# A planner's model: VectorE and GpSimd operations kept apart on a shared path, and time for changes between stream and side products

## The chip, the cores and the metric

The kernel runs on one core of a Trainium2 chip. The metric is the time of one execution on the device, in microseconds (us); less is better.

## The reference

One inference step of a trunk of two layers (DEPTH 2), for a prompt of 256 tokens and one new token of each of 8 running samples, in float32. Cut to what matters here:

```python
def trunk_layer(x, ...):                       # x: (tokens, 2048)
    h = rms_norm(x, norm_w)
    z = h @ w_in                               # columns split among three branches
    y_a, wkv_new = rwkv_time_mix(z_a, ...)     # A: 12 heads of 64, state S (64 x 64) per head
    y_b, kv_new = attention_branch(z_b, ...)   # B: dilated windows, QK norm, rotary, caches
    y_c, pool_new = pool_branch(z_c, ...)      # C: means over 2, 4, 8, 16 rows, small products
    return x + concat(y_a, y_b, y_c) @ w_out, ...

def step(S, inp):                              # inside rwkv_time_mix, one token
    r_t, w_t, k_t, v_t, kk_t, a_t = inp
    sa = einsum('bhvk,bhk->bhv', S, -kk_t)
    S = S * w_t + sa * (kk_t * a_t) + v_t * k_t
    return S, einsum('bhvk,bhk->bhv', S, r_t)
```

For the prompt, `step` is computed in chunks by matrix products; for the samples it is one step on the states that come in as `state_wkv` and leave as `s_wkv`. The outputs are the new rows, the new states and the rows to append to the caches.

## The kernel before

All 264 columns (256 tokens and 8 samples) lie side by side, features on partitions. Layer after layer, `Trunk.stream` brings the weights in tiles `raw` of 512 KB (SyncE's DMA, three buffers). ScalarE rounds each to `hi`, VectorE makes the rest, `lo = raw - hi` (three buffers), and TensorE multiplies: 24 products for each `raw`, `hi` by `xh` and `xl` and then `lo` by `xh`, into two of the three PSUM banks `acc`. After four `raw` a pair of output tiles is complete; VectorE scales the two into `z` (`z<-acc,rstd`), and that frees their banks. These 128x264 products are the *stream*.

All other work of TensorE is called *side* here, and goes through five PSUM banks `a` (line L115 for products, L118 for transposes): the scale of the norm (`row_scale`: the Newton chain `nwt`, `rtok` on VectorE, then `dg` and its products), the chunked recurrence of A (`right`, `iv`, `y`, `uv`, `bt`, `gs`, `st`, `ar`), transposes of `z`, `zv` and `tok`, sums over windows (`kh`), the attention. Side products stand between stream products, so TensorE always has something to do as long as what it needs is there in time.

The samples' step (`a_sample`) cuts the states into 8 pieces `s4` with two buffers. For each piece GpSimd clears it (L789) and starts its loads (L158), does three products (L161) and starts the two stores. VectorE does the multiplications with `arows` (L140), the sum `asa` (L152) and its scale (L144), the rank-one update, and the sum `aos`.

Every engine runs its instructions in a fixed order. That order is set when the kernel is built, by the class `Plan`. It takes the instructions of the program, gives each a duration (`cost`), works out what depends on what, and simulates the five engines with a list of ready instructions for each; the one with the longest chain behind it (`tails`) goes first. Between engines it adds a hand-over time (`HOP`) and, for what does not feed the stream directly, a margin of 350 ns. Then `apply` writes the instructions in the order of the simulated starts. So a number in `Plan` costs nothing by itself and can move instructions on all engines. The two buffers of `s4`, the banks of `acc` and `a` and the other pools are counted in the simulation, and an instruction that lacks one is put aside. Instructions that belong together (`bundle`, a row of small products) are claimed as one.

The plan's durations for GpSimd, the last lines of `cost`, and its use of a DMA started by GpSimd in `run`:

```python
ty = type(i).__name__
return 120 + n * 2.2 if ty == "InstTensorTensor" else 140 + n * 3.2 if ty == "InstTensorCopy" else 50 + n * 0.82
...
free[e] = now + 1050
begin = max(now + 1690, bus_free)
```

Of the kernel before, what the change touches and what calls it, by code (L numbers as in the profile page):

```python
# [103 lines left out]
class Trunk:  # L104
    def __init__(self, ctx, tc, ins, outs, depth=DEPTH):
        self.ctx, self.tc, self.nc, self.ins, self.outs, self.depth = ctx, tc, tc.nc, ins, outs, depth
        self.uid = 0
        self.bundles, self.open = [], None
# [1207 lines left out]
def width(a, first=1):  # L1316
    n = 1
    for _, c in list(a.ap)[first:]:
        n *= c
    return n  # L1320


class Plan:


    def __init__(self, tc, bundles):
        self.tc = tc
        self.tiles = {t.name: t for t in tc.tiles}
        self.block = tc.nc.cur_bb.bb
        self.masks = {}  # L1330
        engine = lambda i: ENGINES.get(str(i.engine).split(".")[-1])
        self.ins = [i for i in self.block.instructions if engine(i) and not type(i).__name__.startswith("BassTilePool")]
        self.eng = [engine(i) for i in self.ins]
        self.n = len(self.ins)
        self.dma = [type(i).__name__ == "InstDMACopy" for i in self.ins]
        self.stream = [type(i).__name__ == "InstMatmult" and self.tiles[list(i.outs)[0].bass_ap.tensor.name].tag.startswith("acc") for i in self.ins]
        self.first = self.stream.index(True)
        self.dur = [self.cost(i, e) for i, e in zip(self.ins, self.eng)]
        self.dependences()
        self.bundle(bundles)  # L1340
        self.rings()
        gone, self.phases = [], []
        for i in self.block.instructions:
            if type(i).__name__.startswith("BassTilePool"):
                op, pool = self.boundary(i)
                if op == "alloc":
                    self.phases += [(pool, g) for g in gone]
                else:
                    gone.append(pool)
# [97 lines left out]
    def cost(self, i, e):  # L1447
        aps = [a for a in list(i.ins) + list(i.outs) if getattr(a, "bass_ap", None) is not None]
        if type(i).__name__ == "InstMatmult":
            n, m = width(aps[0]), width(aps[1])  # L1450
            if "float32r" in str(aps[0].dtype):
                return max(121 * n / 264, 109)
            d = max(n, m) * 0.8333 + 2
            if not getattr(i, "is_transpose", False):
                d = 2 * max(n, m) * 0.8333 + 2
                d *= 0.55 if m <= 32 else 0.72 if m <= 64 else 1
            return d
        if type(i).__name__ == "InstDMACopy":
            return 1050.0
        n = max(width(a) for a in aps)  # L1460
        psum = any(a.bass_ap.tensor.name in self.tiles and self.space(a.bass_ap.tensor.name) == "PSUM" for a in aps)
        wide = [a for a in i.ins if getattr(a, "bass_ap", None) is not None and width(a) > 1]
        thin = sum(1 for a in i.ins if getattr(a, "bass_ap", None) is not None and width(a) == 1)
        if e == "DVE":
            if type(i).__name__ == "InstMemset":
                return 8 + n * 1.04
            fast = type(i).__name__ == "InstTensorScalarPtr" and len(wide) == 1 and not psum
            return 69 + n * (0.52 if fast else 1.042) + (60 if thin else 0)
        if e == "ACT":
            return (51 if psum else 93) + n * 0.834 + (93 * thin if n > 1 else 0)  # L1470
        ty = type(i).__name__
        return 120 + n * 2.2 if ty == "InstTensorTensor" else 140 + n * 3.2 if ty == "InstTensorCopy" else 50 + n * 0.82

    def bus(self, i):
        o = list(i.outs)[0]
        run = min(a.ap[-1][1] * 4 if a.ap[-1][0] == 1 else 4 for a in list(i.ins) + list(i.outs))
        return width(o, 0) * 4 * (1.0 if run >= 512 else 2.0 if run >= 128 else 2.46 if run >= 64 else 8) / 360.0
# [27 lines left out]
    def run(self, factor=1, hop=300, margin=200, batch=0, wait=0, switch=0, quiet=0, lead=1, dyn=()):  # L1505
        n, eng, preds, dma, dur, stream = self.n, self.eng, self.preds, self.dma, self.dur, self.stream
# [37 lines left out]
        free = {e: 0.0 for e in names if e != "SIDE"}  # L1544
        hw = bus_free = now = 0.0
        start, fin, order = [0.0] * n, [0.0] * n, {e: [] for e in free}
        release = []
        last_use = defaultdict(float)
        done, since, side_on, last_stream, forced = 0, None, False, False, None
        claims = {k: [t for t in ts if t in left] for k, ts in self.claim.items()}  # L1550
# [28 lines left out]
        while done < n:  # L1579
            while pending and pending[0][0] <= now + 1e-9:  # L1580
                _, k = heapq.heappop(pending)
# [8 lines left out]
            for e in free:  # L1590
                if free[e] > now + 1e-9 or (e == "SP" and hw > now + 700):
                    continue
                if e == "PE" and forced is not None:
                    k = forced
                elif e == "PE":
# [3 lines left out]
                    k = None  # L1599
                    if h:  # L1600
                        go = side_on or h[0][0] < -2e9 or now - since >= wait or sum(dur[x[1]] for x in h) >= batch
                        if go:
                            k = take(h)
# [3 lines left out]
                    if k is None:  # L1607
                        k = take(ready["PE"])
                        if k is None and h:
                            k = take(h)  # L1610
# [3 lines left out]
                else:  # L1614
                    k = take(ready[e])
# [11 lines left out]
                if dma[k]:  # L1627
                    if e == "SP":
                        hw = max(hw, now) + 470
                        free[e] = now + 60  # L1630
                        begin = max(hw + 650, bus_free)
                    else:
                        free[e] = now + 1050
                        begin = max(now + 1690, bus_free)
                    bus_free = begin + bust[k]
                    fin[k] = bus_free + 908
                else:
                    extra = switch if e == "PE" and stream[k] and not last_stream else 0
                    free[e] = fin[k] = now + dur[k] + extra
                if e == "PE":  # L1640
                    last_stream = stream[k]
                    forced = self.after.get(k)
# [32 lines left out]
            now = min(c)  # L1675
# [68 lines left out]
def build(nc, shapes, depth=DEPTH):  # L1744
    ins = {n: nc.dram_tensor(f"in_{n}", s, F32, kind="ExternalInput").ap() for n, s in shapes.items()}
    outs = {n: nc.dram_tensor(f"out_{n}", s, F32, kind="ExternalOutput").ap() for n, s in _OUTS}
    with tile.TileContext(nc, schedule_with_timeline_sim=True) as tc, ExitStack() as ctx:  # L1747
        trunk = Trunk(ctx, tc, ins, outs, depth)
        trunk.run()
        plan = Plan(tc, trunk.bundles)  # L1750
        plan.run(margin=350, hop=180, factor=0.9, lead=25, quiet=60, dyn=[("a", 2)])
        plan.apply()


# [10 lines left out]
```

## Time and profile before

| what | value |
|---|---|
| median of 3 runs | 1121.6 us (1117.91 to 1131.32) |
| the profiled execution | 1119.54 us |
| its span from the first to the last instruction | 1117.8 us |
| mean granted clock of TensorE | 0.983 |
| TensorE busy | 1052.2 us, 94% |
| VectorE busy | 883.3 us, 79% |
| ScalarE busy | 546.3 us, 49% |
| GpSimd busy | 253.9 us, 23% |

Busy time and waits come from one execution, which lies 2.1 us below the median. Names in a row (`acc<-xh,hi`) are the program's tiles, written one and read ones, without their numbers. In rows of single instructions the time in brackets is idle time of the engine just before, and what ended it. Products of float32 are shown as two records each, so an xcount of 24 in such a row is 12 products. A clock of 1.0 is TensorE's full speed, 0.50 half of it.

### The profile page before, as it was taken

The numbers are of one execution on the slowest core, as the hardware profiler recorded it, in microseconds if no ns is written. First come the engines' busy times: TensorE is split into PE (matmuls) and PEld (weight loads), VectorE is DVE, ScalarE is ACT, GpSimd is POOL, SyncE is SP. The second block draws the span as 40 slices with busy tenths as digits, with TensorE's granted clock in tenths as the row PEclk, the third lists the DMA queues.
The fourth block names the chain that finished last, engine by engine and source line by source line (L and its number), as shares of the span: only waits on it lengthen the run. The fifth ranks groups of instructions, "written<-read, shape, count | busy, mean of one in ns | idle before, by whom it ended". The sixth has DMA issues, their size and how long they took to land. (4 is left out here: it accounts for less than half of the span.)

```text
span 1117.8 us, 24655 instructions
## 1 busy us (share of the span) xinstructions
PE 1052.2 (94%) x9802; PEld 1004.6 (90%) x9802; DVE 883.3 (79%) x1665; ACT 546.3 (49%) x928; POOL 253.9 (23%) x391
## 2 busy tenths in 40 slices
PE   8999999879999999999999999989898899989998
PEld 7899999878899987899999998978888898879998
DVE  7768987698999988865665699668899999787443
ACT  6545533445536545454545464334563474544332
POOL 3202310345532310000121132014453422010000
PEclk9999999889999999999999999998999999999999
DMA  7554478966366894577765545887744578655774
GB/s 253 174 172 150 144 247 235 240 149 199 113 198 192 266 290 136 188 219 224 227 224 170 170 140 177 243 251 189 192 151 133 178 236 286 201 189 181 230 226 143
DMA packets 146652, 221.48 MB, mean 198 GB/s; under 512 B 67441, under 2 KB 100609, under 8 KB 146521
## 3 DMA queue, kind: packets, MB, share of 16 engines
q1 hardware_dynamic: 137272, 193.78, 57.5%
q0 software_dynamic: 9264, 26.13, 7.4%
q8 instruction: 77, 1.26, 0.5%
q14 instruction: 39, 0.31, 0.1%
HBM read 197.47 MB, written 22.95 MB: 197 GB/s over the span
## 5 line engine op out<-in xcount | busy, mean ns | idle before, releaser
L137 ACT ACTIVATE hi<-raw 128x1024 fp32r<-128x1024 f32 (+1 forms) x296 | 310.2, 1048 | 398.1 <-PE acc L321 295.0
L321 PE MATMUL acc<-xh,hi 128*128 128x264 f32 x1824 | 476.4, 292 | 25.0 <-ACT hi L137 10.7
L140 DVE TENSOR_TENSOR lo<-raw,hi 128x1024 fp32r<-128x1024 f32 (+1 forms) x296 | 362.2, 1224 | 153.3 <-ACT hi L137 151.4
L321 PE MATMUL acc<-xl,hi 128*128 128x264 f32 x1824 | 475.3, 292 | 3.8 <-DVE xl L149 3.8
L321 PEld LDWEIGHTS acc<-xh,hi 128*128 128x128 f32 x1824 | 348.9, 191 | 33.7 <-ACT hi L137 11.5
L321 PEld LDWEIGHTS acc<-xl,hi 128*128 128x128 f32 x1824 | 349.8, 192 | 10.3 <-DVE xl L149 4.2
L321 PE MATMUL acc<-xh,lo 128*128 128x264 f32 x1824 | 279.3, 289 | 0.0
L321 PEld LDWEIGHTS acc<-xh,lo 128*128 128x128 f32 x1824 | 243.9, 190 | 3.9 <-issue 1.8
L140 DVE TENSOR_TENSOR z<-acc,rstd 128x264 f32<-128x264 f32 (+1 forms) x112 | 51.3, 463 | 19.3 <-PE acc L321 17.2
L351 POOL COPY zcol<-z 128x9 f32<-128x9 f32 x50 | 23.5, 471 | 146.2 <-DVE z L140 142.0
L321 PE MATMUL acc<-mb,hi 128*128 128x264 f32 x384 | 54.8, 285 | 0.0
L321 PEld LDWEIGHTS acc<-mb,hi 128*128 128x128 f32 x384 | 50.1, 189 | 0.0
L321 PE MATMUL acc<-ml,hi 128*128 128x264 f32 x192 | 48.4, 283 | 0.0
L321 PE MATMUL acc<-mh,hi 128*128 128x264 f32 x192 | 48.2, 283 | 0.0
L321 PEld LDWEIGHTS acc<-mh,hi 128*128 128x128 f32 x192 | 36.1, 188 | 0.0
L321 PEld LDWEIGHTS acc<-ml,hi 128*128 128x128 f32 x192 | 36.0, 188 | 0.0
L321 PE MATMUL acc<-mc,hi 128*128 128x264 f32 x256 | 34.5, 286 | 0.1
L321 PEld LDWEIGHTS acc<-mc,hi 128*128 128x128 f32 x256 | 32.5, 188 | 0.6 <-DVE mc L140 0.5
L158 POOL DMA_DIRECT2D resid<-xs x16 | 8.7, 543 | 102.7 <-DVE xs L140 101.5
L321 PE MATMUL acc<-mh,lo 128*128 128x264 f32 x192 | 31.4, 286 | 0.0
L321 PE MATMUL acc<-mb,lo 128*128 128x264 f32 x192 | 31.1, 284 | 0.0
L158 POOL DMA_DIRECT2D vc<-in_cache_v_w x12 | 9.0, 748 | 96.5 <-PE a L115 61.8
(358 smaller groups left out, 1473.5 us busy)
## 6 DMA issues: line engine op xcount, KB each, us to landing
raw<-in_w_in SPq DMA_DIRECT2D x224, 512.0 KB, 4.4
raw<-in_w_out SPq DMA_DIRECT2D x64, 512.0 KB, 3.5
g_dram<-gs SPq DMA_DIRECT2D x8, 768.0 KB
gs<-g_dram SPq DMA_DIRECT2D x8, 768.0 KB, 6.5
kc<-in_cache_k_w POOLq DMA_DIRECT2D x12, 512.0 KB, 6.8
qb<-q_dram SPq DMA_DIRECT2D x12, 512.0 KB, 3.8
vc<-in_cache_v_w POOLq DMA_DIRECT2D x12, 512.0 KB, 4.7
s<-in_state_wkv POOLq DMA_DIRECT2D x32, 96.0 KB, 3.6
```

The lines of the kernel that those rows point to most:

```text
L137: self.nc.scalar.activation(out, in_, func, **kw)
L140: self.nc.vector.tensor_tensor(out, a, b, op=op)
L158: self.nc.gpsimd.dma_start(out, in_)
L321: self.nc.tensor.matmul(accs[t][:, :T], a[:, k4, cs], b[k], start=first, stop=q == order[3] and k4 == 3 and late)
L351: self.nc.gpsimd.tensor_copy(self.zcol[:, :, a], z[:, NP - 1:T])
```

## The change

Four things in the plan's model are new. `shares` marks the instructions that use a path into SBUF which VectorE and GpSimd have in common: on GpSimd every computing instruction with an operand in SBUF, on VectorE those with two wide operands in SBUF, or a copy or scalar operation from SBUF to SBUF. In the simulation a marked instruction on one of the two engines lasts longer by the time that the other's marked instruction still runs. A stream product behind a side product costs 105 ns more, and a side product behind a stream product 52 ns, unless a bundle begins with it. A DMA that GpSimd starts takes 520 ns of its time instead of 1050. A small GpSimd operation (under 100 elements in a row) costs 120 + 2.2 n ns instead of 140 + 3.2 n or 50 + 0.82 n. The arithmetic and the number of computing instructions are the same; only their order changes.

```diff
         self.dur = [self.cost(i, e) for i, e in zip(self.ins, self.eng)]
+        self.port = [self.shares(i, e) for i, e in zip(self.ins, self.eng)]
         self.dependences()
...
         ty = type(i).__name__
+        if ty == "InstTensorTensor" or n < 100:
+            return 120 + n * 2.2
         return 120 + n * 2.2 if ty == "InstTensorTensor" else 140 + n * 3.2 if ty == "InstTensorCopy" else 50 + n * 0.82
+
+    def shares(self, i, e):
+
+        if e not in ("DVE", "POOL") or type(i).__name__ == "InstDMACopy":
+            return False
+        here = [a for a in i.ins if getattr(a, "bass_ap", None) is not None and a.bass_ap.tensor.name in self.tiles
+                and self.space(a.bass_ap.tensor.name) == "SBUF"]
+        if e == "POOL":
+            return bool(here)
+        wide = [a for a in here if width(a) > 1]
+        to = list(i.outs)[0].bass_ap.tensor.name
+        single = type(i).__name__ in ("InstTensorScalarPtr", "InstTensorCopy") and len(wide) == 1 and self.space(to) == "SBUF"
+        return len(wide) > 1 or single
...
         start, fin, order = [0.0] * n, [0.0] * n, {e: [] for e in free}
+        taken = {"DVE": 0.0, "POOL": 0.0}
...
-                        free[e] = now + 1050
+                        free[e] = now + 520
                         begin = max(now + 1690, bus_free)
...
-                    extra = switch if e == "PE" and stream[k] and not last_stream else 0
+                    extra = 0
+                    if e == "PE" and stream[k] != last_stream:
+                        extra = switch if stream[k] else 0 if k in claims else switch / 2
+                    elif self.port[k]:
+                        extra = max(0.0, taken["POOL" if e == "DVE" else "DVE"] - now)
                     free[e] = fin[k] = now + dur[k] + extra
+                    if self.port[k]:
+                        taken[e] = fin[k]
...
-        plan.run(margin=350, hop=180, factor=0.9, lead=25, quiet=60, dyn=[("a", 2)])
+        plan.run(switch=105, margin=350, hop=180, factor=0.9, lead=25, quiet=60, dyn=[("a", 2)])
```

What that does to the order is shown at three places. The first is VectorE at the start of layer 0, in the Newton chain that leads to `dg` (`lo_105` and `lo_114` are the small parts of two weight tiles, `ss`, `nwt` and `rtok` the chain). Before:

```order
L140 TENSOR_TENSOR lo_105_561<-raw_103_558,hi_104_560 128x1024
L146 TENSOR_SCALAR rtok_60_370<-nwt_61_371 128x3
L140 TENSOR_TENSOR nwt_61_371<-rtok_60_370 128x3
L149 SCALAR_TENSOR_TENSOR nwt_61_371<-nwt_61_371,ss_59_365 128x3
L149 SCALAR_TENSOR_TENSOR rtok_60_370<-nwt_61_371,rtok_60_370 128x3
L140 TENSOR_TENSOR nwt_61_371<-rtok_60_370 128x3
L140 TENSOR_TENSOR lo_114_611<-raw_112_608,hi_113_610 128x1024
L149 SCALAR_TENSOR_TENSOR nwt_61_371<-nwt_61_371,ss_59_365 128x3
L149 SCALAR_TENSOR_TENSOR rtok_60_370<-nwt_61_371,rtok_60_370 128x3
L140 TENSOR_TENSOR nwt_61_371<-rtok_60_370 128x3
```

The same place now:

```order
L146 TENSOR_SCALAR rtok_60_370<-nwt_61_371 128x3
L140 TENSOR_TENSOR nwt_61_371<-rtok_60_370 128x3
L140 TENSOR_TENSOR lo_105_561<-raw_103_558,hi_104_560 128x1024
L149 SCALAR_TENSOR_TENSOR nwt_61_371<-nwt_61_371,ss_59_365 128x3
L149 SCALAR_TENSOR_TENSOR rtok_60_370<-nwt_61_371,rtok_60_370 128x3
L140 TENSOR_TENSOR nwt_61_371<-rtok_60_370 128x3
L149 SCALAR_TENSOR_TENSOR nwt_61_371<-nwt_61_371,ss_59_365 128x3
L149 SCALAR_TENSOR_TENSOR rtok_60_370<-nwt_61_371,rtok_60_370 128x3
L140 TENSOR_TENSOR nwt_61_371<-rtok_60_370 128x3
L140 TENSOR_TENSOR lo_114_611<-raw_112_608,hi_113_610 128x1024
```

Two steps of the chain went ahead of `lo_105` and three ahead of `lo_114`; behind `lo_114` stand two steps instead of five, then `dg`.

The second place is VectorE around the evacuation of the pair of tiles `acc_546`, `acc_547` of layer 0, in the middle of the recurrence and of the samples' pieces. Before:

```order
L152 TENSOR_REDUCE var_463_3282<-gsq_464_3286 128x12
L699 COPY uv_450_3177<-a_468_3320 64x6x64 x2
L140 TENSOR_TENSOR z_560_3993<-acc_546_3871,rstd_66_393 128x264
L140 TENSOR_TENSOR lo_571_4042<-raw_569_4039,hi_570_4041 128x1024
L140 TENSOR_TENSOR z_561_3995<-acc_547_3872,rstd_66_393 128x264
L140 TENSOR_TENSOR s4_336_2206<-s4_336_2206,arows_326_2091 112x512
L140 TENSOR_TENSOR st_470_3348<-a_469_3335,st_454_3221 128x384
L152 TENSOR_REDUCE asa_329_2109<-s4_336_2206 112x8
```

The same place now:

```order
L140 TENSOR_TENSOR s4_336_2206<-asa_329_2109,arows_326_2091 112x512
L146 TENSOR_SCALAR nrs_544_3844<-nwt_545_3848 128x24
L140 TENSOR_TENSOR st_470_3348<-st_470_3348,wc_255_1532 128x384
L140 TENSOR_TENSOR s4_336_2206<-s4_336_2206 112x512
L140 TENSOR_TENSOR nwt_545_3848<-nrs_544_3844 128x24
L146 TENSOR_SCALAR var_463_3282<-var_463_3282 128x12
L140 TENSOR_TENSOR s4_336_2206<-s4_336_2206,arows_326_2091 112x512
L140 TENSOR_TENSOR z_560_3993<-acc_546_3871,rstd_66_393 128x264
L140 TENSOR_TENSOR lo_571_4042<-raw_569_4039,hi_570_4041 128x1024
L140 TENSOR_TENSOR z_561_3995<-acc_547_3872,rstd_66_393 128x264
```

All of `s4_336`'s steps, the update of `st` and steps of a norm (`nss`, `nwt`, `nrs`, `var`) now stand ahead of `z_560`; they stood behind it.

The third place is TensorE at the product of `uv` and `bt` of a chunk, a little later. Before:

```order
L321 MATMUL acc_565_4008<-xh_21_176,lo_574_4072 128x264
L321 MATMUL acc_565_4008<-xh_22_177,lo_574_4072 128x264
L118 MATMUL a_612_4305<-cbase_87,tok_74_409 128x128 x4
L118 MATMUL a_634_4380<-cbase_87,tok_74_409 128x128 x4
L115 MATMUL a_476_3420<-uv_457_3254,bt_456_3253 64x64 x12
L115 MATMUL a_478_3436<-uv_457_3254,gs_466_3303 64x64 x12
L115 MATMUL a_478_3436<-st_470_3348,ar_152_906 64x64 x12
L321 MATMUL acc_565_4008<-xh_23_178,lo_574_4072 128x264
```

The same place now:

```order
L321 MATMUL acc_565_4008<-xh_19_174,lo_571_4042 128x264
L115 MATMUL a_476_3420<-uv_457_3254,bt_456_3253 64x64 x12
L118 MATMUL a_563_4003<-cbase_87,z_561_3995 128x128 x2
L115 MATMUL a_478_3436<-uv_457_3254,gs_466_3303 64x64 x12
L115 MATMUL a_478_3436<-st_470_3348,ar_152_906 64x64 x12
L115 MATMUL a_496_3524<-kh_497_3525,blk_483_3486 128x264
```

The products of this chunk stand one weight tile earlier (by `lo_571` instead of `lo_574`), the sums of `kh` follow at once, and the eight transposes of `tok` are gone from here; they stand later.

## Rows read from the trace of the kernel before

**Rows 1.** The page, part 1: busy us of each engine, share of the span, instructions.

```profile
PE 1052.2 (94%) x9802; PEld 1004.6 (90%) x9802; DVE 883.3 (79%) x1665; ACT 546.3 (49%) x928; POOL 253.9 (23%) x391
```

**Rows 2.** Busy time by stretch: us, PE, PEld, DVE, ACT, POOL busy (instructions), PEclk, DMA share, GB/s.

```profile
216.00:284.80 68.80, 60.02 (x984) 55.88 (x983) 61.56 (x94) 34.51 (x66) 35.40 (x45) 0.95 0.62 178
284.80:461.00 176.20, 166.37 (x1496) 154.22 (x1495) 162.05 (x368) 90.35 (x186) 46.93 (x68) 0.99 0.63 199
...
763.00:830.10 67.10, 60.03 (x987) 55.99 (x986) 61.17 (x94) 34.55 (x67) 35.16 (x45) 0.95 0.67 187
830.10:1010.00 179.90, 167.56 (x1509) 155.54 (x1508) 164.67 (x360) 92.14 (x186) 45.33 (x66) 0.99 0.63 196
```

**Rows 3.** TensorE's waits: its line, what it waited for, us in total, times, longest.

```profile
PE acc L321 <- ACT hi L137: 10.7, 4, 3.8
PE acc L321 <- DVE z L140: 7.1, 8, 2.2
...
PE a L115 <- DVE right L149: 5.2, 2, 2.6
PE a L118 <- DVE zv L140: 4.9, 2, 2.8
PE a L115 <- DVE dg L144: 4.5, 2, 2.5
...
PE a L115 <- DVE zv L140: 3.2, 2, 1.7
```

**Rows 4.** VectorE's timeline at the start: start us, length us, engine, line, operation.

```profile
41.40 1.81 DVE L149 SCALAR_TENSOR_TENSOR nwt<-nwt,ss 128x3 f32<-128x3 f32 x1
```

**Rows 5.** VectorE's timeline around and behind the evacuation of `acc_546`, layer 0.

```profile
284.76 0.43 DVE L140 TENSOR_TENSOR z<-acc,rstd 128x264 f32<-128x264 f32 x1 [0.40 <-PE acc L321]
...
286.84 0.91 DVE L140 TENSOR_TENSOR s<-s,arows 112x512 f32<-112x512 f32 x1
...
290.39 1.17 DVE L144 TENSOR_SCALAR asa<-asa 112x8 f32<-112x8 f32 x1
...
296.61 0.16 DVE L144 TENSOR_SCALAR asa<-asa 112x8 f32<-112x8 f32 x1
...
316.27 0.68 DVE L152 TENSOR_REDUCE aos<-s 112x8 f32<-112x512 f32 x1
```

**Rows 6.** GpSimd's timeline at the same place.

```profile
290.24 1.29 POOL L161 TENSOR_TENSOR s<-s 112x512 f32<-112x512 f32 x1
```

**Rows 7.** TensorE's timeline: stream and side, side products of a chunk, stream alone.

```profile
218.59 0.39 PE L321 MATMUL acc<-xh,hi 128*128 128x264 f32 x1
218.82 0.38 PE L118 MATMUL a<-cbase,z 128*128 128x128 f32 x2
218.96 0.37 PE L321 MATMUL acc<-xl,hi 128*128 128x264 f32 x1
...
285.96 0.92 PE L115 MATMUL a<-uv,bt 128*64 128x64 f32 x24
...
288.35 0.87 PE L118 MATMUL a<-cbase,bk 128*128 128x128 f32 x6
...
325.28 0.28 PE L321 MATMUL acc<-xh,hi 128*128 128x264 f32 x1
325.40 0.29 PE L321 MATMUL acc<-xl,hi 128*128 128x264 f32 x1
```

**Rows 8.** Busy time by stretch where PEclk was 0.50; the sum of five.

```profile
304.36:307.77 3.41, 3.41 (x65) 3.23 (x60) 3.41 (x9) 0.51 (x1) 0.00 (x0) 0.50 0.49 143
...
850.49:853.91 3.42, 3.42 (x64) 3.20 (x59) 3.42 (x9) 0.52 (x1) 0.00 (x0) 0.50 0.37 102
sum 20.49, PE 20.29 PEld 19.28 DVE 19.22 ACT 3.08 POOL 5.24; mean PE 4.06 PEld 3.86 DVE 3.84 ACT 0.62 POOL 1.05
```

**Rows 9.** All instructions of one tile, `out_s_wkv`: ns min/median/max, first and last start.

```profile
L158 POOL DMA_DIRECT2D out_s_wkv<-s x32: 502/512/553, 227.2 to 880.3; - x32
```

## The prediction, made before the changed kernel had run

> **What bounds the kernel now.** I read the page first, then the busy time by stretch, then TensorE's waits, then the timelines at the places that the new order touches. TensorE is busy for 1052.2 of 1117.8 us [rows 1], so 65.6 us of idle time is all that a new order can remove, apart from stretches at half clock and the cost of changing between kinds of product. VectorE looks comfortable at 79% [rows 1], but that is a mean: from 216.0 to 284.8 us it is busy for 61.56 of 68.80 us, and in the same place of layer 1 for 61.17 of 67.10 us, and TensorE is least busy just there (8.8 and 7.1 us idle) [rows 2]. There VectorE, in its fixed order, is what ends the waits: of TensorE's waits for products of VectorE, `z` has 7.1 us, `right` 5.2, the two groups for `zv` 4.9 and 3.2 [rows 3]. The longest single item, 10.7 us for `hi`, is ScalarE behind a weight tile that has just landed; the order of the weight loads on SP is the same in both kernels at those places, so that item stays.
>
> **What the change is worth, part by part.** It removes and adds no instruction. What it does to the time is what another order does, so each term is a place where the order differs. The profiled execution took 1119.54 us (span 1117.8), 2.1 us below the median of 1121.6; I sum against 1119.54 and give the forecast in the same terms.
>
> *Start.* The tile `dg` needs a Newton chain of tiny VectorE operations, and TensorE waited 2.5 us for it in layer 0 (the longest of `dg` in [rows 3]). The last five of the chain ran behind `lo_114` and met two GpSimd products there: the first of them took 1.81 us [rows 4] where its neighbours take 0.16. In the new order three of the five, that one among them, stand ahead of `lo_114`, and two stay behind it. The gain lies between 0 (the last two and `dg` meet the same products instead) and 2.5 us (the whole wait). I take the one blocked operation, 1.81 − 0.16: **−1.7 us**.
>
> *Up to the pinch.* I call pinch the point where VectorE evacuates `acc_546` into `z_560` (284.76 us in the trace, and its like at 830 us in layer 1). 21 VectorE instructions that stood behind it stand ahead of it now, most of them steps of the sample pieces `s4_335` and `s4_336`; none went the other way. The first ran at 286.84 us and the last at 316.27 us [rows 5]; their 21 durations add up to 13.5 us. Rows there overlap the next by 0.08 us each, so they hold the engine for 11.8 us. Of that 2.1 us was contention, half of it in one of them: 1.17 us at 290.39 against 0.16 at 296.61 [rows 5]. It began 0.15 us after GpSimd's product of 290.24 us and ended with it [rows 6]. If the plan does keep such pairs apart, 9.7 us is left; if not, 11.8.
>
> On TensorE 48 products come ahead of the same point. 36 of them are the `uv,bt`, `uv,gs` and `st,ar` of one chunk; the like of these took from 285.96 to 288.35 us [rows 7], 2.4 us for as many. The other 12, transposes and pooled sums, are between 0.07 us (two transposes held TensorE from 218.82 to 218.96 us [rows 7]) and twice that: 0.8 to 1.7 us. So 3.2 to 4.1 us of TensorE's later work is done before the pinch. If VectorE recovers none of its idle time, the pinch comes 9.7 − 4.1 = 5.6 to 11.8 − 3.2 = 8.6 us late for the work then left. If it fills all its idle time (68.80 − 61.56 = 7.2 and 67.10 − 61.17 = 5.9 us [rows 2]), the end is 5.6 − 7.2 = −1.6 to 8.6 − 5.9 = +2.7 us. The idle time there is in short pieces behind `hi` and `acc`, and a sample step that is ready can fill about every second one. I take 5.6 less half of the mean idle of 6.6: **+2.3 us a layer**, between −1.6 and +8.6.
>
> *After the pinch.* VectorE has those 9.7 us less to do. Two waits for `zv` and the longest of `z` lie here: 4.9 + 3.2 + 2.2 = 10.3 us for both layers [rows 3], 5.2 a layer. All could go. But by the later point `acc_869` the new order has 52 VectorE instructions, some 16 us by their rows, and 12.5 us of TensorE's side products ahead that were behind, attention's above all, so the room is partly sold again: between 0 and −5.2, taken at half, **−2.6 us a layer**.
>
> *Clock.* In the four stretches TensorE's granted clock was 0.50, its lower level, for 20.5 us in all, which cost 10.2 [rows 8]. One such window lasts 3.4 us and costs 1.7. Those at 304.36 and 850.49 us begin less than 2 us behind the two waits for `zv` (2.1 and 2.8 us [rows 3]). Where the wait goes, I expect the window to go: 0 to −3.4 us, and half, **−1.7**, in line with half of the waits. Others follow the wait for `right`, which only 19 stream matmuls cover now instead of 23, so I leave them.
>
> *Changes of kind.* A stream matmul that is followed by a side product starts it 0.23 us later (218.59 to 218.82 us) instead of the 0.12 between stream matmuls (325.28 to 325.40); side to stream costs nothing more (218.82 to 218.96 for two) [rows 7]. The plan now charges 52 ns for the first and 105 for the second, so its sign is the wrong way round, but it only has to make runs longer. The order has 433 such changes instead of 453, 10 fewer of the dear kind: 10 × 0.1 = **−1.0 us**.
>
> *DMA issue on GpSimd.* The plan's 1050 ns becomes 520. All 32 stores of `s4` took 502 to 553 ns [rows 9], beside a VectorE that was busy nearly throughout, so the new value is right here and the order built on it is feasible: nothing added.
>
> The Trainium skill has a rule against this part (SBUF — State Buffer, "SBUF: two separate sides"): a DMA issued by GpSimd gets no descriptors while VectorE holds the shared ports in its faster mode, and one of about 620 ns takes about 3100 there. By it an issue would come up to 2.5 us later than the plan believes, an estimate from that page, the sample pieces would not be ready in their turn, and the time would be that of the slower rival below. The trace disagrees so far: the longest of the 32 issues took 553 ns [rows 9].
>
> Sum: −1.7 + 2 × 2.3 − 2 × 2.6 − 1.7 − 1.0 = −5.0, so **1114.5 us**; I write 1114. With every bound on one side it would be −2.5 − 3.2 − 10.3 − 3.4 − 1.0 = −20.4 (1099) or +17.2 (1137). Five terms do not all fall together, so this case's own range is 1102 to 1129.
>
> **Rivals.** *The plan becomes true (faster).* If what made the two stretches of each layer idle is mostly that GpSimd blocked VectorE at moments unknown to the plan, an order that knows it loses most of those waits, not half of a few. TensorE idles 8.8 + 9.8 + 7.1 + 12.3 = 38.0 us in these four stretches [rows 2]. Two thirds is 25 us, and with the waits two thirds of the 10.2 us lost to half clock there go [rows 8], 7 us: 32 us in all, **1088 us**. For it: blocked rows of 1 us and more stand right ahead of TensorE's waits for `zv`. Against it: much of the waiting follows chains with no GpSimd in them (`right`, `hi`), and VectorE is nearly full whatever the order.
>
> *VectorE's line becomes the pinch (slower).* Engines run in order. The sample steps now stand ahead of `z_560` and of the `lo` tiles behind it; when one waits for GpSimd's product or for a landing, the stream stands still, because `acc` has three buffers and the next pair of tiles needs `z_560`. If none of VectorE's idle time is recovered, each layer pays 8.6 us, nothing comes back later, and the two longer waits each bring a half-clock window of 1.7 us: 17.2 + 3.4 = 20.6, **1140 us**. It decides where a sample step ahead of `z_560` is not ready when `acc_546` ends; the plan's margins say it is, and before it was the other way round (VectorE waited 0.40 us for `acc` there [rows 5]).
>
> *Nothing that counts.* The waits move to other operations and add up to the same: **1120 us**, as before.
>
> **How the numbers follow.** The forecast 0.50, faster rival 0.18, slower rival 0.17 (0.02 of it by way of late issues), nothing 0.15. A range of 8 in 10 takes in the forecast and the third whole and about half of either rival: **1091 to 1138 us**. A difference of 2% is about what a measurement of this kernel can tell from no change (runs from 1117.91 to 1131.32); that is below 1099 or above 1144. Below lies the faster rival and a little of the forecast's edge, 0.19; above only the end of the slower rival, 0.09; between them 0.72.
>
> **What would show it.** In the profile of the changed kernel: the wait for `dg` at 46 us under 1 us; `z_560` 0 to 9 us later against the stream matmuls done; fewer VectorE rows of `asa` and `s` above 1 us; the waits for `zv` shorter and the window at about 304 us gone; GpSimd's issues still near 510 ns. The forecast is wrong if sample steps on VectorE show waits for GpSimd or DMA ahead of `z_560` (slower), or if TensorE's idle time in the four stretches falls below 20 us (faster).

## The result, and the profile after

The changed kernel is a little slower: median 1131.5 us (1126.82 to 1135.57) against 1123.02 us for the kernel before on the same chips, ratio 1.0076, 95% interval 1.0053 to 1.0099. One of the 15 runs of the kernel before took 1915.98 us, far from all others, and does not count in the ratio. The profiled execution has a span of 1125.0 us, 7.2 more than that of before. First the page of the changed kernel, part 1 [rows 1]:

```profile
PE 1057.5 (94%) x9802; PEld 1008.1 (90%) x9802; DVE 885.1 (79%) x1665; ACT 544.3 (48%) x928; POOL 263.8 (23%) x391
```

TensorE's idle time is 67.5 us (1125.0 − 1057.5), 1.9 more than the 65.6 of before, and its busy time is 5.3 us more: most of what was lost shows as longer products. To see where, I cut both traces at the same stream products (between the cuts a few stand in another order): from the start of product 1200 to the last of the pair `acc_546`, `acc_547` (the pinch), and from there to product 2700; then the like in layer 1. Busy time by stretch, columns as in [rows 2]; the kernel before:

```profile
192.80:285.10 92.30, 79.71 (x1124) 75.36 (x1123) 73.25 (x109) 45.26 (x78) 40.37 (x52) 0.93 0.74 197
285.10:468.50 183.40, 173.57 (x1555) 161.43 (x1555) 168.49 (x379) 94.57 (x193) 46.93 (x68) 0.99 0.64 199
740.60:829.20 88.60, 77.69 (x1118) 73.43 (x1117) 72.08 (x108) 44.20 (x77) 39.79 (x52) 0.94 0.77 205
829.20:1021.40 192.20, 179.87 (x1610) 167.84 (x1610) 174.10 (x379) 98.90 (x196) 45.33 (x66) 0.99 0.62 194
```

The changed kernel:

```profile
192.20:290.80 98.60, 83.93 (x1206) 78.56 (x1206) 84.95 (x127) 48.94 (x86) 58.25 (x66) 0.93 0.67 181
290.80:472.70 181.90, 172.61 (x1471) 160.64 (x1470) 157.35 (x362) 90.61 (x185) 33.50 (x54) 0.97 0.62 200
745.30:842.50 97.20, 83.24 (x1202) 78.67 (x1200) 85.35 (x123) 48.05 (x85) 56.79 (x64) 0.93 0.69 183
842.50:1028.70 186.20, 177.76 (x1528) 165.08 (x1527) 161.64 (x364) 94.28 (x188) 33.41 (x55) 0.99 0.63 201
```

Up to the pinch the stretches grew by 6.3 and 8.6 us, and VectorE works 11.7 and 13.3 us more in them (73.25 to 84.95, 72.08 to 85.35). TensorE works 4.2 and 5.6 us more there too, so its idle time grew by 2.1 and 3.0 us (12.6 to 14.7, 10.9 to 14.0). Behind the pinch the stretches shrank by 1.5 and 6.0 us. So VectorE did run ahead, TensorE waited longer, and only part of what it had done ahead came back. TensorE's waits in the changed kernel [rows 3]:

```profile
PE acc L321 <- ACT hi L137: 11.4, 7, 2.6
PE acc L321 <- DVE z L140: 10.1, 9, 2.9
PE acc L321 <- DVE compb L140: 9.3, 4, 4.9
PE a L115 <- DVE uv L699: 7.3, 7, 2.5
PE a L115 <- DVE dg L144: 4.9, 2, 2.5
...
PE a L118 <- DVE zv L140: 0.2, 1, 0.2
```

In the kernel before, two of these, which [rows 3] leaves out, were shorter:

```profile
PE acc L321 <- DVE compb L140: 6.9, 3, 2.9
PE a L115 <- DVE uv L699: 1.3, 2, 0.7
```

The waits for `right` and `zv` are gone (13.3 us), and `uv`, `z` and `compb` have taken their place (11.4 us more). The longest, 4.9 us for `compb` (the tail of the same evacuation as `z`), shows how. VectorE's timeline in layer 1 ahead of it, in the changed kernel [rows 5]:

```profile
794.33 2.47 DVE L140 TENSOR_TENSOR s<-s,arows 112x512 f32<-112x512 f32 x1
796.72 2.44 DVE L140 TENSOR_TENSOR s<-asa,arows 112x512 f32<-112x512 f32 x1
799.08 0.67 DVE L152 TENSOR_REDUCE asa<-s 112x8 f32<-112x512 f32 x1
799.68 0.58 DVE L140 TENSOR_TENSOR z<-acc,rstd 128x256 f32<-128x256 f32 x1
800.11 0.17 DVE L140 TENSOR_TENSOR compb<-acc,rstd 128x8 f32<-128x8 f32 x1
```

GpSimd at the same time [rows 6], and the stream product that waited:

```profile
794.98 1.26 POOL L161 TENSOR_TENSOR s<-s 112x512 f32<-112x512 f32 x1
796.21 1.18 POOL L161 TENSOR_TENSOR kh<-k,kh 128x264 fp32r<-128x264 f32 x1
797.36 1.25 POOL L161 TENSOR_TENSOR s<-s,arows 112x512 f32<-112x512 f32 x1
...
800.42 0.56 PE L321 MATMUL acc<-xh,hi 128*128 128x264 f32 x1 [4.87 <-DVE compb L140]
```

Two sample steps, 0.68 us each when undisturbed, take 2.47 and 2.44 us while GpSimd's products run; with the sum behind them they stood behind `z` in the kernel before. Now `z` stands behind them in the fixed order, and the stream behind `z`. The wait costs twice: a half-clock window follows it. Those of the changed kernel in the recurrences, two of them and the sum of all seven [rows 8]:

```profile
302.00:308.80 6.80, 6.44 (x80) 5.64 (x79) 5.73 (x8) 2.93 (x6) 0.60 (x1) 0.50 0.38 117
...
800.40:803.80 3.40, 3.38 (x15) 3.35 (x15) 3.40 (x6) 1.06 (x1) 2.62 (x2) 0.50 0.21 36
...
sum 37.40, PE 34.76 PEld 32.39 DVE 34.65 ACT 13.37 POOL 20.68; mean PE 4.97 PEld 4.63 DVE 4.95 ACT 1.91 POOL 2.95
```

In the same two recurrences the kernel before was at half clock for 30.7 us. Behind layer 0's, the changed kernel has one more such window:

```profile
370.30:373.70 3.40, 3.40 (x18) 3.40 (x17) 2.02 (x4) 1.05 (x2) 1.51 (x3) 0.50 1.01 368
```

The other runs agree: the mean granted clock is 0.976 over the 15 runs of the changed kernel, and 0.981 to 0.982 over each of four sets of runs of the kernel before, taken beside the experiments. By an estimate from these figures the clock cost at most 27 us (0.024 × 1131.5) against 20 to 22, so 5 to 7 of the 8.5 us can be clock.

All operations of `asa`'s scale and of the stores [rows 9] in the changed kernel, ns min/median/max, and `asa`'s scale in the kernel before:

```profile
L144 DVE TENSOR_SCALAR asa<-asa x16: 157/1006/3919, 213.3 to 853.4; 112x8 f32<-112x8 f32 x16
...
L158 POOL DMA_DIRECT2D out_s_wkv<-s x32: 502/516/553, 223.4 to 870.4; - x32
```

```profile
L144 DVE TENSOR_SCALAR asa<-asa x16: 157/312/1169, 217.4 to 866.3; 112x8 f32<-112x8 f32 x16
```

To go by this operation, VectorE is blocked by GpSimd more than before, not less: the median of `asa`'s scale was 0.31 us before and is 1.0 now. The order explains that. With the wait in `run` for marked operations taken out, the plan gives the same order, on TensorE, VectorE and GpSimd alike. `shares` compares the memory space with `"SBUF"`, while the tiles' own name for it is `"SB"`, so it marks no instruction at all. Leaving out the new costs of small GpSimd operations leaves VectorE's order as it is too, and changes 36 of 8638 places in TensorE's order and 8 of 391 in GpSimd's; that was not run alone. So VectorE's new order comes from two parts: the charges between stream and side products, and the 520 ns.

### The profile page after: what moved, and what is told of

It is laid out like the page before. It is cut to its first block, busy times and chain, and to the rows that moved or that the text cites. A ratio compares the mean times of both kernels' runs of the same rounds, so it can differ in the third digit from the quotient of the medians.

```text
span 1125.0 us, 24664 instructions
## 1 busy us (share of the span) xinstructions
PE 1057.5 (94%) x9802; PEld 1008.1 (90%) x9802; DVE 885.1 (79%) x1665; ACT 544.3 (48%) x928; POOL 263.8 (23%) x391
## 5 line engine op out<-in xcount | busy, mean ns | idle before, releaser
L321 PE MATMUL acc<-xh,hi 128*128 128x264 f32 x1824 | 473.9, 291 | 32.0 <-ACT hi L137 11.4
L321 PE MATMUL acc<-xh,lo 128*128 128x264 f32 x1824 | 285.5, 292 | 0.6 <-DVE lo L140 0.6
L321 PEld LDWEIGHTS acc<-xh,lo 128*128 128x128 f32 x1824 | 247.0, 192 | 6.8 <-issue 2.8
L140 DVE TENSOR_TENSOR z<-acc,rstd 128x264 f32<-128x264 f32 (+1 forms) x112 | 51.2, 464 | 16.5 <-PE acc L321 14.2
L351 POOL COPY zcol<-z 128x9 f32<-128x9 f32 x50 | 18.5, 369 | 146.6 <-DVE z L140 144.9
L140 DVE TENSOR_TENSOR s<-s,arows 112x512 f32<-112x512 f32 x32 | 25.4, 796 | 5.6 <-DMA rat<-rat_dram 3.5
```

The lines of the kernel that those rows point to most:

```text
L140: self.nc.vector.tensor_tensor(out, a, b, op=op)
L321: self.nc.tensor.matmul(accs[t][:, :T], a[:, k4, cs], b[k], start=first, stop=q == order[3] and k4 == 3 and late)
L351: self.nc.gpsimd.tensor_copy(self.zcol[:, :, a], z[:, NP - 1:T])
```

## The experiments

Every kernel is the whole computation; only numbers of the plan differ, and so the order. Ratios are to the kernel before on the same chip. I count VectorE instructions that stand ahead of a pair's evacuation and stood behind it in the kernel before, less those that went the other way: at `z_560` (the pinch) and at `z_763`, the first pair behind layer 0's recurrence. "Recurrence" is the time from stream product 1200 to 1820 and its like in layer 1, together, in the profiled execution, against 257.3 us before.

| kernel | at `z_560` | at `z_763` | recurrence, us | ratio (interval) |
|---|---|---|---|---|
| port_marked_alone | −25 | −46 | −19.6 | 1.0192 (1.0161 to 1.0222) |
| port_half_alone | −8 | −31 | −12.2 | 0.9992 (0.9969 to 1.0015) |
| port_quarter_alone | −6 | −23 | −14.4 | 0.9904 (0.9873 to 0.9935) |
| port_marked | −19 | −18 | −0.2 | 1.0020 (0.9993 to 1.0047) |
| port_half | 12 | −2 | −16.8 | 0.9951 (0.9924 to 0.9978) |
| margin355 | 0 | 9 | −0.3 | 0.9995 (0.9970 to 1.0020) |
| port_quarter | 12 | 12 | +2.1 | 1.0026 (1.0001 to 1.0050) |
| dma520_alone | 10 | 13 | −0.3 | 0.9977 (0.9951 to 1.0004) |
| switch_alone | 7 | 22 | −1.1 | 0.9996 (0.9974 to 1.0017) |
| charges_52 | 8 | 24 | +8.9 | 1.0036 (1.0009 to 1.0063) |
| stream128 | 17 | 38 | +7.7 | 1.0144 (1.0109 to 1.0179) |
| charges_dma785 | 9 | 40 | +13.9 | 1.0055 (1.0030 to 1.0080) |
| charges_swapped | 19 | 45 | +11.3 | 1.0095 (1.0063 to 1.0127) |
| the changed kernel | 21 | 47 | +9.5 | 1.0076 (1.0053 to 1.0099) |
| changed_margin355 | 21 | 47 | +4.6 | 1.0116 (1.0088 to 1.0144) |
| changed_hold | 39 | 50 | +9.4 | 1.0110 (1.0074 to 1.0147) |
| stream134 | 44 | 59 | | 1.0284 (1.0245 to 1.0323) |

**The two parts alone, the marking made to work, and a control.** The theory was that what stands ahead of `z_560` costs in proportion; the rival, that any other order scatters by as much.

```diff
# dma520_alone, on the kernel before
-                        free[e] = now + 1050
+                        free[e] = now + 520
# port_marked, on the changed kernel (twice)
-self.space(...) == "SBUF"
+self.space(...) == "SB"
# margin355, on the kernel before
-plan.run(margin=350,
+plan.run(margin=355,
```

> The plan with the GpSimd DMA issue at 520 ns and nothing else of the change. Ledger theory (what stands ahead of z_560 on VectorE sets the loss of the recurrence stretch, 4.7 us a layer for 21 instructions): 10 stand ahead here, so about 2.2 us a layer slower, no gain at the start since that order is the old one: 1.004 of before, some 1127 us. Redraw theory (any changed number of the plan gives another order, and its time scatters by half a per cent whatever the ledger says): anywhere from 0.995 to 1.01, with losses in other places than the recurrence stretch.

> The plan with the charges for changes between stream and side products and nothing else. Ledger theory: 7 instructions ahead of z_560, so 1.6 us a layer, less 1 to 2 us at the start, whose new order comes from this part: about 1.002 of before. Redraw theory: 0.995 to 1.01. If the charges are what costs (they are larger for side to stream, which in the trace of before cost nothing), this kernel alone shows the whole 0.76%.

> The changed kernel with the name of the memory space in shares() corrected, so that operations are marked at all (as it stands the test compares with a name that no tile has, and no instruction is marked). 19 VectorE instructions then stand behind z_560 that stood ahead of it in before. Ledger theory: the recurrence stretch is no slower than before and waits for VectorE fall: 0.99 to 1.0 of before. Rival, VectorE is full in that stretch whatever the order: what is not done ahead is done behind, the chain of the samples ends later, and the time stays between 1.003 and 1.012. Fewer VectorE rows of asa above 1 us in either case.

> The kernel before with one number of the plan moved a little, the margin from 350 to 355 ns: a control for how far any redraw of the order moves the time. Ledger theory: VectorE's order up to z_560 is the old one, so the recurrence stretch stays within 1 us and the whole within 0.3%. Redraw theory: it moves by 0.4% or more, in either direction, as much as the change did.

Neither part alone costs anything that can be measured, and together (with the small costs) they cost 0.8%. The proportional theory falls with the first of them: 10 instructions ahead, and no loss in the recurrence. The charges alone don't even save changes between the two kinds: 457 against 453 before. The control fits the ledger, not the scatter, although the two intervals of dma520_alone and margin355 are too wide to tell 0.3%. port_marked came out between its two theories: its recurrences are as long as before, its time is not clearly longer, and, against what I expected, the median of `asa`'s scale is 1.0 us there too.

**Is the loss one of this order, of the sign of the charges, or of the sample pieces?** The threshold theory: nothing is lost up to VectorE's idle time, everything beyond it.

```diff
# charges_swapped, on the changed kernel
-                        extra = switch if stream[k] else 0 if k in claims else switch / 2
+                        extra = 0 if stream[k] else switch
# changed_hold: VectorE's first step on s4_336 (and s4_1437) not before acc_547 is done
+            held[point].append(first)
+            count[first] += 1
```

> The changed kernel with the charges turned round: 105 ns for a side product behind a stream product, which is the change that cost 0.1 us in the trace of before, and nothing for a stream product behind a side one. 19 VectorE instructions ahead of z_560 instead of 21. Threshold theory (what stands ahead of the stream's steps on VectorE costs nothing up to its idle time of some 6 us a layer, about 10 to 14 instructions, and everything beyond): the loss is nearly the whole one, 1.005 to 1.008 of before. Wrong-charge theory (the loss comes from charging the wrong kind of change): 0.995 to 1.001. Redraw theory: anything from 0.995 to 1.01.

> The changed kernel with the margin at 355 ns instead of 350: a redraw of its own order, that leaves 21 instructions ahead of z_560 and changes the later stretches, of layer 1 above all. Threshold theory: the loss of the recurrence stretches stays, 1.005 to 1.010 of before. Redraw theory: the loss is an accident of one order and goes, at least by half, below 1.004.

> The changed kernel, in which the plan may start VectorE's work on s4_336 (and its like of layer 1) only when the stream has finished acc_547. The planner fills the place with other work: 39 instructions then stand ahead of z_560 instead of 21. Threshold theory: more beyond the idle time, so slower than the changed kernel, 1.010 or more of before. Theory of the sample pieces (it is those steps, with their waits for GpSimd, that hold the line): faster than the changed kernel, under 1.005. Redraw theory: no order between the two.

> The kernel before with nothing but the marking of shared operations, with the name of the memory space corrected: 25 VectorE instructions stand behind z_560 that stood ahead of it, and up to 87 later on. Threshold theory: the stream's steps have VectorE to themselves, so the recurrence stretch gets faster, and what was put off must fit behind: 0.99 to 1.0. Rival, VectorE is full whatever the order: the recurrence's own chain comes later, and the time is 1.003 or more of before.

Three more orders with 19 to 39 instructions ahead lose 1.0 to 1.2%: the loss is no accident of one order, the direction of the charges doesn't matter, and with the steps of `s4_336` behind the pinch the planner fills the place with others and loses as much. Two of the three lost more than I expected, and not all of it in the recurrences: these hold 11.3 of the 14.7 us by which the profiled span of charges_swapped is longer, 9.4 of changed_hold's 18.9, and only 4.6 of changed_margin355's 14.3. The rest is not explained. The fourth missed its expectation in an instructive way. With the full wait charged, VectorE's side work goes behind, and the recurrence gets 19.6 us shorter, but the time is 1.9% longer. Its profile, busy time of the stretch behind layer 0 (272.1 us long before, 305.3 here), and TensorE's longest waits in it:

```profile
449.20:754.50 305.30, 282.30 (x2274) 269.71 (x2273) 214.20 (x395) 136.08 (x210) 44.93 (x84) 0.94 0.59 186
```

```profile
PE a L118 <- DVE os L152: 11.1, 3, 4.4
PE a L115 <- POOL comp L444: 2.9, 1, 2.9
PE acc L321 <- ACT mb L137: 2.2, 2, 1.1
```

What was put off isn't done when the stream has read all of the layer's input weights, and the output projection waits for the attention (`os`, then `mb`). So there are two ways to lose.

**TensorE slower in the model, and half doses.**

```diff
# stream134 (and 128), on the kernel before
-                return max(121 * n / 264, 109)
+                return max(134 * n / 264, 109)
# charges_dma785, on the changed kernel
-                        free[e] = now + 520
+                        free[e] = now + 785
# port_half (0.5) and port_quarter (0.25), on port_marked; "alone": without charges and 520 ns
-                        extra = max(0.0, taken["POOL" if e == "DVE" else "DVE"] - now)
+                        extra = 0.5 * max(0.0, taken["POOL" if e == "DVE" else "DVE"] - now)
# charges_52, on the changed kernel
-plan.run(switch=105,
+plan.run(switch=52,
```

> The kernel before with one duration in the plan changed: a stream product counts 134 ns instead of 121. TensorE is slower in the model, and 44 VectorE instructions stand ahead of z_560 that stood behind it, with no charge for changes and the DMA issue at 1050 ns. Threshold theory (any time added to TensorE in the model lets VectorE's side work run ahead of the stream, and beyond VectorE's idle time the stream pays): the recurrence stretches of the two layers lose 8 us or more together, 1.008 of before or more. Rival, the loss needs the DMA issue at 520 ns or the charges: within 0.3% of before.

> The changed kernel with the GpSimd DMA issue at 785 ns, half way: 9 VectorE instructions ahead of z_560, but 40 and 42 at two points of the later stretch, as many as in the changed kernel. Threshold theory with the place in the recurrence stretch: no loss there, 0.997 to 1.003 of before. Rival, what stands ahead in the later, attention stretch costs the time: 1.006 or more.

> The changed kernel with the marking made to work and half the wait charged: VectorE's order against the stream stays near that of before (12 ahead of z_560, 12 behind at the next pair, mixed later). Threshold theory: neither loss, 0.994 to 1.002 of before, and with the 520 ns the better end if knowing the shared path is worth anything. Rival, charging the shared path hurts at any size: 1.003 or more.

> The kernel before with the marking made to work and half the wait charged, nothing else: 8 VectorE instructions behind z_560 and up to 48 behind later, about half of the full charge. If the cost of the other side is work that spills out of the layer's recurrence and attention (the full charge lost 1.9%, after it had gained 20 us in the recurrence stretches), half the shift should keep part of the gain and little of the spill: 0.99 to 1.005. If every put-off instruction costs: about 1.009.

One number that makes TensorE slower in the model, with nothing of the change, loses 2.8%. That this is the same mechanism at a larger dose is not shown: its one profile, of the slowest of its six runs, has recurrences only about 5 us longer, of 44 us in all. charges_dma785 missed: 9 ahead at `z_560` and yet 13.9 us lost in the recurrence. So the count at the pinch isn't what decides; that at the recurrence's end, 40, fits. port_half is faster than both kernels, port_half_alone as expected.

> The changed kernel with the marking made to work and a quarter of the wait charged: 14 VectorE instructions ahead of z_560, 12 at z_763. Rule at z_763: the recurrence stretches of both layers together within 4 us of before, the whole 0.995 to 1.002. Accident of single orders: no relation.

> The kernel before with a quarter of the wait charged and nothing else: 6 behind at z_560, 23 behind at z_763. Rule at z_763: recurrence stretches 5 to 14 us shorter together; the whole 0.992 to 1.0, since some of it is given back behind. Accident of single orders: no relation.

> The changed kernel with the charges at half size (52 and 26 ns): 9 ahead of z_560, 24 at z_763. Rule at z_763: recurrence stretches within 4 us of before, the whole 0.997 to 1.004, so most of the loss of the changed kernel is gone. Accident of single orders: no relation.

> The kernel before with a stream product counted at 128 ns instead of 121, nearer to what the trace shows (0.125 us): 20 ahead of z_560, 38 at z_763. Rule at z_763: recurrence stretches 4 to 10 us longer together, the whole 1.004 to 1.012, although the plan's duration is truer. Accident of single orders: no relation.

Three of the four came out as the count at `z_763` says, all three a little beyond the time that I expected; charges_52 missed in the recurrence (+8.9 us with 24 ahead) though its time is near. **port_quarter_alone** is the version to keep: 1111.55 us median, 0.9904 of before. It is the best of sixteen orders, so a part of that may be luck. Its VectorE at the place where the changed kernel waited 4.9 us:

```profile
785.35 1.21 DVE L140 TENSOR_TENSOR lo<-raw,hi 128x1024 fp32r<-128x1024 f32 x1
786.48 0.59 DVE L140 TENSOR_TENSOR z<-acc,rstd 128x256 f32<-128x256 f32 x1
786.92 0.17 DVE L140 TENSOR_TENSOR compb<-acc,rstd 128x8 f32<-128x8 f32 x1
786.98 0.61 DVE L140 TENSOR_TENSOR z<-acc,rstd 128x256 f32<-128x256 f32 x1
787.42 0.18 DVE L140 TENSOR_TENSOR compb<-acc,rstd 128x8 f32<-128x8 f32 x1
787.48 0.67 DVE L152 TENSOR_REDUCE asa<-s 112x8 f32<-112x512 f32 x1
```

and its two recurrences by stretch, with the clock at 0.99 instead of 0.93 and 0.95; the kernel before first:

```profile
192.80:322.50 129.70, 114.40 (x1529) 108.64 (x1528) 110.33 (x177) 62.07 (x104) 62.25 (x78) 0.93 0.65 178
...
740.60:868.10 127.50, 113.10 (x1529) 107.45 (x1528) 110.29 (x177) 61.58 (x103) 57.62 (x75) 0.95 0.66 181
```

```profile
194.90:316.70 121.80, 109.98 (x1528) 103.89 (x1527) 105.83 (x162) 61.58 (x104) 64.09 (x73) 0.99 0.69 187
...
738.00:859.10 121.10, 109.16 (x1528) 103.66 (x1526) 107.56 (x161) 61.17 (x103) 66.77 (x73) 0.99 0.70 188
```

The three sample steps that the changed kernel has ahead of this `z` stand behind it here. Of the 14.4 us that the recurrences are shorter, 5.9 are idle time of TensorE; the rest is busy time, at the higher clock. It is not a matter of less blocking: the median of `asa`'s scale is 0.73 us in this kernel, longer than the 0.31 of before.

## Why the prediction was wrong

**The bound** was read rightly: VectorE in its fixed order, in the recurrence stretches. The gain of port_quarter_alone lies there too: 14.4 us, of which it gives 3.5 back elsewhere.

**Up to the pinch.** I had "9.7 us is left" for VectorE, from a plan that keeps contended pairs apart, less 4.1 us of TensorE's work, less half of VectorE's idle time: +2.3 us a layer. The stretches grew by 6.3 and 8.6 us; TensorE did 4.2 and 5.6 us more work in them (3.2 to 4.1 foreseen; of the 5.6, 1.7 is one more window at half clock), and its idle time grew by 2.1 and 3.0 us. So the size came out, in part by luck: VectorE's extra work measured 11.7 and 13.3 us, the value for no pair kept apart or more, since `shares` marks nothing, and 5.4 us (19.1 to 13.7) and 4.7 us (16.5 to 11.9) of its idle time were filled, more than the 3.3 I had taken.

**After the pinch** I expected −2.6 us a layer, besides the 4.1 us of TensorE's work already done. TensorE's idle time fell by 0.5 us (9.8 to 9.3) and 3.9 us (12.3 to 8.4), a little less than that in sum; its busy time fell by only 1.0 and 2.1 us. My reason, that VectorE "has those 9.7 us less to do", holds for VectorE (11.1 and 12.5 us less), but its idle time grew by most of that (14.9 to 24.6, 18.1 to 24.6). TensorE idles for only some 5% of these stretches, so room on VectorE buys little there.

**Start.** The gain was at its lower bound, nothing, where I had −1.7. The last two of the chain and `dg` met the same GpSimd products, now at 39 to 43 us; VectorE in the changed kernel [rows 4]:

```profile
39.41 1.81 DVE L149 SCALAR_TENSOR_TENSOR nwt<-nwt,ss 128x3 f32<-128x3 f32 x1
...
41.45 1.91 DVE L144 TENSOR_SCALAR dg<-cbase,rtok 128x128 f32<-128x128 f32 x2
```

TensorE still waits 2.4 us for `dg` there, and from stream product 0 to 1200 the time is 181.3 us against 180.8.

**Clock: the step that failed.** I expected half of two windows to go (−1.7): where the wait goes, the window goes. The wait for `zv` went and the window stayed, because a wait for `uv` of 2.5 us stands at 301.8 instead; the wait of 4.9 us for `compb` has one of 3.4 us behind it. In the two recurrences half clock lasts 37.4 us, against 20.5 [rows 8] and two windows of 6.8 and 3.4 us ahead of those in before, 30.7: 6.7 us more, which cost 3.3. The sign was wrong: I had counted the windows of the waits that go and none for the waits that come. With it and the changes of kind below, I had TensorE's busy time 2.7 us lower, and it rose by 5.3: that is 8.0 of the 12.2 us between −5.0 and the +7.2 of the profiled spans. Over the whole execution half clock lasts 44.7 us against 38.6, which is 3.1 of the 5.3; what makes the other 2.2 is not known. TensorE's idle time, −2.3 in the forecast and +1.9 measured, makes the other 4.2 us, most of it at the start (−1.7 and +1.0).

**Changes of kind** went from 453 to 433 as counted; a gain of 1 us is too small to be seen. The 0.1 us for one rested on a single row. Over the trace of before, where TensorE neither waits nor is at half clock, a side product of L115 starts 0.21 us behind a stream product (median of 107), but a transpose of L118 0.12 (median of 93), as a stream product does. **DMA issue**: 502 to 553 ns, right, and dma520_alone loses nothing. The rule of the Trainium skill that I weighed (SBUF — State Buffer, "SBUF: two separate sides") is about a DMA that waits for its descriptors, and I took that to lengthen the issue. No issue of a store in any run here was longer than 560 ns. From issue to landing a store took 2.1 to 5.8 us in before and 2.1 to 7.9 in the changed kernel; no run separates a wait for descriptors in that.

**The rivals.** The slower rival had the mechanism: steps of the samples ahead of the stream's on VectorE, waiting for GpSimd, with `z` behind them. Its price of 20.6 us was more than double the 8.5 measured, because VectorE did fill idle time and part of the work done ahead came back. I gave it 0.17 only, and took the plan's margins as a reason against it. That the change doesn't do what it says should have been a rival: `shares` asks for a name that the rest of the class never uses, and the order could have told it.

**What stays open.** The count at `z_763` orders the kernels well at its ends (40 and more: 4.6 to 13.9 us lost where it was read; −23 and less: 12 to 20 gained), not in the middle: 24 ahead lost 8.9 us, 22 none, and −18 (port_marked) gained nothing. At the like place in layer 1 the count is within 4 of this, but for switch_alone: 39 there, and its recurrence is 3.0 us longer in layer 1 and 4.1 shorter in layer 0. Against that, changed_margin355 has 47 in both layers and lost 5.0 us in layer 1 alone. VectorE's and TensorE's orders move together in all of these kernels; VectorE's alone was not tried, so how much of the loss is TensorE's own order isn't separated; nor is how much of the loss is waits and how much the clock that follows them. Stretches are from one execution each, and the runs of one kernel lie 6 to 16 us apart; margin355, with the same VectorE instructions ahead of the pinch as before, agrees with it within 0.3 us in the recurrence, but differs by 9 us behind it.

## What to carry to other kernels

A list scheduler keeps its engines busy in its own model, so a number that slows the bounding engine there (a charge for changes, a longer product time) can let the other engines' side work run ahead of the steps that feed it; where a queue runs in order, the bounding engine can pay for that on the chip, as the wait for `compb` shows. When an order takes waits away, count those that it brings, and the clock behind them. Before believing that a term of such a model does something, compare the order with and without it; here the first term in the title had no effect, and two side terms that are harmless alone cost 0.8% together. Then look for the dose: the shared path charged at a quarter gained 1% (alone; with the other parts nothing), at the full wait it lost 1.9%, because work that is put off must still be done before the stream's next dependent phase.

## What the runs showed of the hardware

A longer duration for a stream product made a worse plan: 128 ns instead of 121 lost 1.4%. I had called it truer, which it is not clearly: over the trace of before, where TensorE neither waits nor is at half clock, a stream product starts 121 ns behind the one ahead by the median and 125 by the mean.

A small VectorE operation can be passed over by several GpSimd instructions in a row. `asa`'s scale, 0.16 us alone, in the changed kernel, and GpSimd beside it:

```profile
236.75 3.92 DVE L144 TENSOR_SCALAR asa<-asa 112x8 f32<-112x8 f32 x1
```

```profile
236.56 1.06 POOL L158 DMA_DIRECT2D s<-in_state_wkv  x2
237.64 1.05 POOL L161 TENSOR_TENSOR s<-arows 112x512 f32<-112x512 f32 x1
238.65 0.74 POOL L161 TENSOR_TENSOR kh<-k,kh 128x264 fp32r<-128x264 f32 x1
239.35 1.28 POOL L161 TENSOR_TENSOR s<-s 112x512 f32<-112x512 f32 x1
```

It begins during two DMA issues and ends with the third product behind them, at 240.6 us. No model here, the corrected marking included, charges that: there an operation waits for one product, and none for a DMA issue.
